# A hybrid S5 and attention block: the S5 output taken with 128 stationary columns instead of 32

## The chip, the core and the metric

The kernel runs on one core of one Trainium2 chip. The metric is the device time of one execution in microseconds, the median of several runs; shorter is better. TensorE (PE, its weight loads PEld), VectorE (DVE), ScalarE (ACT), GpSimd (POOL) and SyncE (SP, which here only issues the weight loads) each take their own instructions in order and wait for each other by semaphores.

## What is computed

One decoder block on 256 tokens of width 2048, all in float32. A modulation of six vectors is made from a conditioning vector, the input is normalised and modulated, and one projection gives u, q, k and v of 1024 channels each. u goes through a diagonal complex state space layer (S5): 64 groups of 16 channels with 64 complex states each. q, k and v go through an attention of 8 heads with three dilated windows merged. Both halves are joined in an output projection, and a SwiGLU feed forward layer follows. What matters here is the S5 layer:

```
bu = einsum('bsgc,gnc->sbgn', u, Bbar)              # complex
h[t] = abar * h[t-1] + bu[t]                        # per group and state, over 256 tokens
y = Re(einsum('sbgn,gcn->bsgc', h, C)) + d * u
y = gelu(y);  ssm_out = y * sigmoid(y @ w_glu)
```

## The kernel before

**The dense products.** Every weight matrix comes in tiles of 256 rows by 512 columns (512 KB), loaded by SyncE into a ring of six buffers (`load`, line 106) in the order of use. ScalarE casts each tile to its high part (`whi`, line 131) and VectorE subtracts to get the low part (`wlo`, line 133); there are three buffers of each. TensorE then makes three products for each piece, high by high, high by low and low by high (`mm_tok`, line 150). The modulation weights go through the same ring of raw tiles and are used uncast, by TensorE (line 225) or, for one gate and one block, by VectorE (lines 260 and 280).

**The stages.** First the modulation and u^T, then q, k, v with the S5 layer and the rest of the modulation alongside (the loop over `step()`), then the GLU of the S5 output (line 911), the output projection, the second norm, and the feed forward layer.

**The S5 layer.** It is worked in eight batches m of 128 channels, eight groups of 16. Time is cut into 64 blocks j of four tokens (four phases i or r). `U` holds the input with 4 phases x 32 channels on the 128 partitions, for each quarter Q of a batch's channels and each block j. `ssm_tables(m)` makes the constant operands of a batch. `ssm_batch(m)` does the work: TensorE brings the input to the states (`S`, line 690), ScalarE copies `S` out of PSUM (line 693), VectorE turns the states, runs the scan over the 64 blocks (line 705) and turns them back into `hp`; TensorE makes the output y from two sources, the input within the block through the triangular table `T` (line 720) and the state before the block through `Vt` (line 724); then ScalarE copies y out of PSUM (line 728) and squares it (line 729), and ScalarE and VectorE finish GELU and write the high and low parts of `yT` (lines 731 to 739). In the old form each phase r and quarter Q has a product of its own with 32 stationary columns, placed on the 32 partitions of that quarter, so that y has the channels of the batch in order on its partitions.

**Order.** The program order of the parallel stage is written out by generators: after each weight tile, `step()` advances the modulation and the lanes of S5 batches (two lanes, even and odd m) and of attention heads. The order of instructions on TensorE, VectorE, ScalarE and GpSimd is then made by the framework's planner from that program order, its priorities and its own cost model; the casts of line 131 have a raised priority. Only SyncE's order is the program's. Pools that matter: PSUM tiles `ms` have three buffers (y, S, transposes, scores), the accumulators `acc` two, and the working tiles `wk` of the S5 lanes (written by the tables and the batches) two. The tile `vt`, into which v is copied (line 785), takes the place of an earlier table tile.

Of the kernel before, what the change touches and what calls it, by code (L numbers as in the profile page):

```python
# [7 lines left out]
F32 = mybir.dt.float32  # L8
# [43 lines left out]
# columns of the array of small operands  # L52
# [9 lines left out]
def body(tc, sm, tabs, bc, brow, x, wada, wg2, win, wglu, wout, wgate, wup, wdown, out):  # L62
# [26 lines left out]
    def rsqrt(pool_, v, n, tag):  # L89
        """v [128, n] -> 1/sqrt(v) (integer first guess, Newton)"""  # L90
# [18 lines left out]
    # weights in the order of their use, split into high and low parts, read ahead  # L109
# [30 lines left out]
    def split(dst, src):  # L140
        """dst [128, ch, 2, n] f32r <- src [128, ch, n] as high and low parts"""
        A.copy(dst[:, :, 0], src)
        V.tensor_tensor(out=dst[:, :, 1], in0=src, in1=dst[:, :, 0].bitcast(F32), op=ALU.subtract)

    def mm_tok(ps, lhs, hl, j, first, last, ts_=range(2)):
        """ps [128, 2, 512] += lhs(h, t)^T @ w"""
# [5 lines left out]
    # ================= scope 1: up to the second norm =================  # L152
# [8 lines left out]
    def WK(name):  # L161
        """working tile of one S5 lane: three parts of 2 KB"""
# [14 lines left out]
    c7 = p1.tile([128, 16, 7], F32, name="c7")        # columns 3 - i .. 6 - i: c in place i  # L177
# [4 lines left out]
    sel = p1.tile([128, 4], F32, name="sel")          # place i of every quadrant  # L182
    V.reduce_sum(sel, ident.rearrange("p (q r) -> p r q", q=4)[:, 0:4], axis=AX.X)

# [5 lines left out]
    # a part: (kind, first group of 128 columns, groups); kinds shift1, scale1, gate1, shift2, scale2  # L190
# [19 lines left out]
    def ada_stream(sets):  # L210
        """generator: one tile a step; the parts of a set share a bank, and are finished while the next set runs"""
        pend = None
        for parts in sets:
            ps = ada_ps
            last = len(parts) - 1
            for i, (kind, g0, ng) in enumerate(parts):
                w = ng * 128
                nk = 1024 // w                     # groups of 128 rows in a tile
# [50 lines left out]
    def ada_dve():  # L269
        """generator: blocks of the second modulation on VectorE, one tile a step"""  # L270
# [70 lines left out]
    pw = p1.tile([128, 5, 3, 32], F32, name="pw")      # abar^0..4: re, im, -im  # L341
    rho4 = SC("rho4")
    el = p1.tile([128, 6, 2, 32], F32, name="el")      # exp(i 4 theta 2^l)
    bct = P8([128, 4, 32, 16], "bct")

    def s5_consts():
# [3 lines left out]
        def horner(o, x, cs_):  # L350
            """o = cs[0] + x (cs[1] + x (...))"""
            ts(o, x, cs_[-1], None, ALU.mult)
            for c_ in cs_[-2:0:-1]:
                stt(o, o, c_, x, ALU.add, ALU.mult)
            ts(o, o, cs_[0], None, ALU.add)
# [4 lines left out]
        def vexp(o, x, kf, r):  # L360
            """exp(x) as 2^k times a polynomial; 0 below the normal range"""
# [29 lines left out]
        tt(tmpb, tmpb, th, ALU.mult)                   # sin of the half angle  # L391
# [4 lines left out]
        ts(tmpb, tmpb, 2.0, None, ALU.mult)            # sin  # L396
        ts(tmpc, tmpc, -2.0, 1.0, ALU.mult, ALU.add)   # cos
# [6 lines left out]
        def csq(ore, oim, re, im):  # L404
            """o = (re + i im)^2"""
# [22 lines left out]
        # Bbar = ((abar - 1) / a) B  # L428
# [16 lines left out]
        ts(bct[:, 3], bct[:, 3], -1.0, None, ALU.mult)       # C as its conjugate  # L445
# [14 lines left out]
    def te_parts(m):  # L460
        """T [(i ch), Q, r, ch'] and E [e, Q, j] of the channels of m"""
# [5 lines left out]
    def ssm_rot(mp):  # L467
        """E_j = exp(i 4 theta j) of two batches"""
# [25 lines left out]
    def ssm_tables(m):  # L494
        """tables of the channels 128 m .. 128 m + 127 (4 pairs of groups)"""
# [3 lines left out]
        Bm = bct[:, 0:2, pr]                       # [128, 2, 4, 16]  # L499
        Cm = bct[:, 2:4, pr]  # L500
        wv = P8([128, 2, 4, 2, 4, 32], "wv")       # 0: W1^T [(i ch), (Q, e), state]  1: V [Q, e, tau, ch]
        wv_t[m] = wv
        wst = T4([128, 4, 2, 4, 32], "wst")        # Q, e, i, ch
        wk = WK("wkt")
        T, _ = te_parts(m)
        Tf = T.rearrange("p q r c -> p (q r c)")   # room for the steps to K
# [3 lines left out]
        Vt = wv[:, 1]                              # [128, Q, e, tau, 32]  # L510
# [3 lines left out]
        dn = wk(2, 4, 2, 4, 16)                    # Q, e, i, ch  # L514
        # W stage: block diagonal abar^(3-i) Bbar
# [9 lines left out]
        for ps_, cs_ in HV:  # L525
            A.copy(wst[ps_, :, :, :, cs_].rearrange("p q e i c -> p (q e i) c"), dn[ps_].rearrange("p q e i c -> p (q e i) c"))
            for e in range(2):
                A.copy(c0[ps_, :, e, cs_], Cm[ps_, e])             # C as its conjugate
        yield 1.6
        # V_tau, tau = 1 .. 4  # L530
# [13 lines left out]
        # K_tau = Re(C abar^tau Bbar), tau = 3 - i  # L544
# [15 lines left out]
        # Toeplitz part [(i ch), Q, r, ch'] = K_(r - i), i <= r, d on the diagonal  # L560
# [3 lines left out]
        for i in range(3):                         # r = 2: i = 0..2 <- partitions 32 (i + 1)  # L564
# [76 lines left out]
    def u_copy(b):  # L641
        """U [(i, 32 ch), m, Q, j] = u[4 j + i, 128 m + 32 Q + ch]"""
# [38 lines left out]
    def ssm_batch(m):  # L681
# [35 lines left out]
        for Q in range(4):  # L717
            yq = y[32 * Q:32 * Q + 32]
            for r in range(4):
                PE.matmul(yq[:, r], lhsT=T[:, Q, r], rhs=U[:, m, Q], start=r == 0, stop=False, skip_group_check=True,  # L720
                          tile_position=(0, 32 * Q))
            for r in range(4):
                for e in range(2):
                    PE.matmul(yq[:, r], lhsT=Vt[:, Q, e, r], rhs=hp[:, e, Q], start=False, stop=e == 1, skip_group_check=True,  # L724
                              tile_position=(0, 32 * Q))
# [504 lines left out]
```

## Time and profile before

| | |
|---|---|
| time, median of 3 runs | 1269.51 us (1268.36 to 1269.92) |
| span of the profiled execution, first to last instruction | 1262.8 us (a time of its own beside the span is not given) |
| TensorE busy | 1229.4 us (97%) |
| VectorE busy | 790.1 us (63%) |
| ScalarE busy | 569.4 us (45%) |
| GpSimd busy | 25.5 us (2%) |
| moved by DMA | 302.74 MB, mean 240 GB/s |

The busy shares are means over the whole span; a stage can have another limit than the mean shows. A busy TensorE is not TensorE at its peak, since matmuls are pipelined and their ends are modelled, so the starts of neighbouring instructions tell more than their lengths. TensorE's granted clock is at its full level from 37 us on. A float32 product with float32 operands (as S and y) is recorded as two passes, so its counts are twice those of the code.

### The profile page before, as it was taken

How to read it: one execution, taken by the hardware profiler on the slowest of the kernel's cores; microseconds unless marked ns; L12 is line 12 of the kernel's file. 1: busy time of each engine (PE TensorE's matmuls, PEld its weight loads, DVE VectorE, ACT ScalarE, POOL GpSimd, SP SyncE). 2: the span in 40 equal slices, each digit the busy share in tenths (PEclk: the TensorE clock that was granted, in tenths of full speed). 3: DMA queues.
4: the chain of work that ended last, by engine and by line, in shares of the span. 5: the costliest groups of instructions: out<-in, count | busy, mean ns of one | idle time of the engine just before them, and what ended most of it. 6: DMA issues, size and time to landing. Idle time of an engine off the chain costs nothing.

```text
span 1262.8 us, 18076 instructions
## 1 busy us (share of the span) xinstructions
PE 1229.4 (97%) x6884; PEld 961.9 (76%) x6884; DVE 790.1 (63%) x1389; ACT 569.4 (45%) x859; POOL 25.5 (2%) x50
## 2 busy tenths in 40 slices
PE   5889999999999999999999999999999999999998
PEld 2556557676789877688888888888888878888886
DVE  7994354666778999865655665665555444545443
ACT  4663363445456555554344443444434443333432
POOL 1110000000000000000000000000000000000000
PEclk9999999999999999999999999999999999999999
DMA  9889967767687899567777777777766656767662
GB/s 376 268 294 350 347 217 266 249 235 260 219 323 237 264 333 326 203 190 240 240 240 229 233 247 232 238 238 226 244 199 192 187 166 197 208 194 212 191 211 67
DMA packets 83032, 302.74 MB, mean 240 GB/s; under 512 B 9248, under 2 KB 9664, under 8 KB 82304
## 3 DMA queue, kind: packets, MB, share of 16 engines
q1 hardware_dynamic: 80784, 294.69, 71.6%
q10 hardware_dynamic: 1728, 4.38, 0.9%
q0 software_dynamic: 432, 2.51, 0.5%
q8 instruction: 54, 0.88, 0.3%
q14 instruction: 34, 0.28, 0.1%
HBM read 299.44 MB, written 2.10 MB: 239 GB/s over the span
## 4 chain that ended last, share of the span: by engine, by line
PE 83%; DVE 8%; DMA 5%; issue 2%; ACT 2%; DVEq 0%; ACTq 0%
PE ff L150 38%; PE dn L150 14%; PE qkv L150 9%; PE ada L225 5%; PE dnl L150 5%; DMA raw<-wada 4%; PE uacc L600 3%; DVE wlo L133 2%; PE y L724 2%; DVE gate L260 1%; PE q L150 1%; PE S L690 1%; PE y L720 1%; PE atp L1106 1%; ACT whi L131 1%
## 5 line engine op out<-in xcount | busy, mean ns | idle before, releaser
L133 DVE TENSOR_TENSOR wlo<-raw,whi 128x1024 fp32r<-128x1024 f32 x365 | 445.6, 1222 | 323.4 <-ACT whi L131 322.4
L131 ACT CAST whi<-raw 128x1024 fp32r<-128x1024 f32 x365 | 384.3, 1053 | 517.8 <-PE ff L150 263.7
L150 PE MATMUL ff<-whi,h2T 128*128 128x512 f32 x1408 | 437.1, 390 | 0.7 <-DVE h2T L1026 0.5
L150 PEld LDWEIGHTS ff<-whi,h2T 128*128 128x128 f32 x1408 | 264.0, 188 | 56.8 <-ACT h2T L1025 1.0
L150 PE MATMUL ff<-wlo,h2T 128*128 128x512 f32 x704 | 274.1, 389 | 0.0
L150 PE MATMUL dn<-whi,aT 128*128 128x512 f32 x528 | 163.4, 390 | 0.0
L150 PEld LDWEIGHTS ff<-wlo,h2T 128*128 128x128 f32 x704 | 132.2, 188 | 27.0
L150 PEld LDWEIGHTS dn<-whi,aT 128*128 128x128 f32 x528 | 99.1, 188 | 21.1 <-ACT whi L131 0.2
L150 PE MATMUL qkv<-whi,hT 128*128 128x512 f32 x320 | 107.7, 402 | 0.0
L150 PE MATMUL dn<-wlo,aT 128*128 128x512 f32 x264 | 103.1, 391 | 0.0
L225 PE MATMUL ada<-raw,c 128*4 128x256 f32 (+1 forms) x736 | 87.5, 467 | 14.7 <-DVE c L179 9.8
L150 PEld LDWEIGHTS qkv<-whi,hT 128*128 128x128 f32 x320 | 60.0, 188 | 25.9 <-issue 9.9
L1084 DVE SCALAR_TENSOR_TENSOR gate<-raw,cs,gate 128x1024 f32<-128x1024 f32 x32 | 41.1, 1284 | 53.5 <-DMA raw<-wg 53.5
L150 PE MATMUL qkv<-wlo,hT 128*128 128x512 f32 x160 | 63.3, 395 | 0.0
L600 PE MATMUL uacc<-hT,whi 128*128 128x256 f32 x256 | 53.0, 300 | 4.7 <-ACT whi L131 2.3
L150 PEld LDWEIGHTS dn<-wlo,aT 128*128 128x128 f32 x264 | 49.6, 188 | 10.6 <-issue 0.5
L150 PE MATMUL dnl<-whi,aT 128*128 128x512 f32 x176 | 54.5, 389 | 0.0
L600 PEld LDWEIGHTS uacc<-hT,whi 128*128 128x128 f32 x256 | 40.8, 195 | 17.5 <-issue 8.8
L260 DVE SCALAR_TENSOR_TENSOR gate<-raw,cs,gate 128x512 f32<-128x512 f32 x64 | 47.7, 747 | 5.0 <-DMA raw<-wada 4.5
L225 PEld LDWEIGHTS ada<-raw,c 128*4 128x4 f32 x736 | 12.8, 85 | 44.6 <-issue 17.4
L600 PE MATMUL uacc<-hT,wlo 128*128 128x256 f32 x128 | 38.1, 298 | 1.6 <-DVE wlo L133 1.6
L150 PEld LDWEIGHTS dnl<-whi,aT 128*128 128x128 f32 x176 | 33.0, 188 | 7.1 <-DVE o L333 0.2
(312 smaller groups left out, 1259.2 us busy)
## 6 DMA issues: line engine op xcount, KB each, us to landing
raw<-wada SPq DMA_DIRECT2D x160, 512.0 KB, 5.2
raw<-wgate SPq DMA_DIRECT2D x88, 512.0 KB, 4.4
raw<-wup SPq DMA_DIRECT2D x88, 512.0 KB, 4.3
raw<-wdown SPq DMA_DIRECT2D x88, 512.0 KB, 4.2
raw<-win SPq DMA_DIRECT2D x64, 512.0 KB, 5.0
raw<-wout SPq DMA_DIRECT2D x32, 512.0 KB, 4.6
raw<-wg SPq DMA_DIRECT2D x32, 512.0 KB, 4.3
raw<-wglu SPq DMA_DIRECT2D x8, 512.0 KB, 4.7
```

What stands on the lines that cost most here:

```text
L131: A.copy(hi, raw)
L133: V.tensor_tensor(out=lo, in0=raw, in1=hi.bitcast(F32), op=ALU.subtract)
L150: PE.matmul(ps[t] if type(ps) is list else ps[:, t], lhsT=lhs(a, t), rhs=w[:, j], start=first and n == 0, stop=last and n == 2)
L225: PE.matmul(ps[32 * q:32 * q + 4, 0:w], lhsT=c7[:, kc, 3 - i:7 - i], rhs=wt[:, j * w:(j + 1) * w], start=i == 0 and kc < 4, stop=i == last ...
L260: V.scalar_tensor_tensor(out=gb, in0=wt[:, j], scalar=cs[:, 2 * h + j:2 * h + j + 1], in1=gb, op0=ALU.mult, op1=ALU.add)
L600: PE.matmul(uacc[b][:, c], lhsT=wt[:, j, w], rhs=h[:, j, a], start=(kc == 0 and n == 0 and c % 2 == 0), stop=(kc == 15 and n == 2), skip_g ...
L690: PE.matmul(S[:, e, Q], lhsT=wv[:, 0, Q, e].rearrange("p i c -> p (i c)"), rhs=U[:, m, Q], start=True, stop=True)
L720: PE.matmul(yq[:, r], lhsT=T[:, Q, r], rhs=U[:, m, Q], start=r == 0, stop=False, skip_group_check=True, tile_position=(0, 32 * Q))
L724: PE.matmul(yq[:, r], lhsT=Vt[:, Q, e, r], rhs=hp[:, e, Q], start=False, stop=e == 1, skip_group_check=True, tile_position=(0, 32 * Q))
L1084: V.scalar_tensor_tensor(out=g, in0=wt, scalar=cs[:, k:k + 1], in1=g, op0=ALU.mult, op1=ALU.add)
L1106: PE.transpose(tp[:, k, t * 128:(t + 1) * 128], sg[:, t, (k2 * 2 + k) * 128:(k2 * 2 + k + 1) * 128], ident)
```

## The change

Comments are removed, and in `ssm_batch` the S5 output is made and copied in another way:

```diff
         y = ms([128, 4, 64], "y")
         for Q in range(4):
-            yq = y[32 * Q:32 * Q + 32]
-            for r in range(4):
-                PE.matmul(yq[:, r], lhsT=T[:, Q, r], rhs=U[:, m, Q], start=r == 0, stop=False, skip_group_check=True,
-                          tile_position=(0, 32 * Q))
-            for r in range(4):
-                for e in range(2):
-                    PE.matmul(yq[:, r], lhsT=Vt[:, Q, e, r], rhs=hp[:, e, Q], start=False, stop=e == 1, skip_group_check=True,
-                              tile_position=(0, 32 * Q))
+            PE.matmul(y[:, Q], lhsT=T[:, Q].rearrange("p r c -> p (r c)"), rhs=U[:, m, Q], start=Q == 0, stop=False, skip_group_check=True)
+            for e in range(2):
+                PE.matmul(y[:, Q], lhsT=Vt[:, Q, e].rearrange("p r c -> p (r c)"), rhs=hp[:, e, Q], start=False, stop=e == 1,
+                          skip_group_check=True)
         ysb, t1 = wk(1, 64, 4), wk(2, 64, 4)
-        A.copy(ysb, y.rearrange("p r j -> p j r"))
+        for r in range(4):
+            for Q in range(4):
+                A.copy(ysb[32 * Q:32 * Q + 32, :, r], y[32 * r:32 * r + 32, Q])
         A.activation(t1, ysb, AF.Square)
```

The four phases of a quarter are now one stationary operand of 128 columns (the tables lie that way already), so a product gives 4 phases x 32 channels on the partitions, and the quarter goes into the free dimension. Per batch 48 products become 12. Since the steps behind want the channels on the partitions and the phase next to the block, the one ScalarE copy of 128 partitions by 256 becomes 16 copies of 32 partitions by 64, each from the 32 partitions of phase r to the 32 partitions of quarter Q, written with a stride of four elements. Everything after the copies is unchanged, and so is the order in which the program issues the stages.

## Rows read from the trace of the kernel before

**Rows 1.** The chain of work that ended last, of the whole kernel: its shares by engine, then by line.

```profile
PE 83%; DVE 8%; DMA 5%; issue 2%; ACT 2%; DVEq 0%; ACTq 0%
PE ff L150 38%; PE dn L150 14%; PE qkv L150 9%; PE ada L225 5%; PE dnl L150 5%; DMA raw<-wada 4%; PE uacc L600 3%; DVE wlo L133 2%; PE y L724 2%; DVE gate L260 1%; PE q L150 1%; PE S L690 1%; PE y L720 1%; PE atp L1106 1%; ACT whi L131 1%
```

**Rows 2.** The three stretches around the change: start and end in us, its length, busy time of PE, PEld, DVE, ACT and POOL, each with its number of instructions, the granted TensorE clock (1.00 is full speed), the busy share of the DMA engines and what they moved.

```profile
178.00:385.00 207.00, 206.99 (x1658) 150.08 (x1657) 137.98 (x363) 97.45 (x232) 8.09 (x13) 1.00 0.72 252
385.00:525.00 140.00, 137.17 (x719) 113.60 (x718) 129.18 (x227) 75.83 (x121) 0.53 (x1) 1.00 0.85 289
525.00:1263.00 738.00, 732.41 (x3264) 604.07 (x3262) 406.64 (x381) 307.04 (x320) 0.50 (x1) 1.00 0.68 208
```

**Rows 3.** The TensorE passes that make the S5 output y: count, duration in ns (least/median/most), first and last start in us, form of the operands.

```profile
L724 PE MATMUL y<-wks,wv x512: 219/219/243, 204.0 to 378.2; 128*32 128x64 f32 x171
...
L720 PE MATMUL y<-U,te x256: 219/219/243, 203.5 to 377.3; 128*32 128x64 f32 x128
```

**Rows 4.** TensorE in order of time, around one S product and around the second pair of S5 outputs: start and length in us, line, operation, number of instructions merged.

```profile
229.76 2.00 PE L690 MATMUL S<-U,wv 128*128 128x64 f32 x16
231.57 0.47 PE L150 MATMUL qkv<-whi,hT 128*128 128x512 f32 x1
...
252.32 0.61 PE L720 MATMUL y<-U,te 128*32 128x64 f32 x8
...
261.78 0.50 PE L150 MATMUL qkv<-whi,hT 128*128 128x512 f32 x1
```

**Rows 5.** ScalarE: four groups of instructions by form (busy us, mean ns of one, idle time before), and then two places of its order of time.

```profile
L646 ACT COPY U<-uacc 32x256 f32<-32x256 f32 x22 | 8.0, 364 | 1.7 <-PE uacc L600 1.4
...
L693 ACT COPY wks<-S 128x512 f32<-128x512 f32 x8 | 4.7, 586 | 7.2 <-PE S L690 7.2
...
L524 ACT COPY wkt<-bct 128x64 f32<-128x64 f32 x16 | 3.3, 242 | 2.4 <-DVE te L333 1.6 <-DVE yT L739 0.7
...
L728 ACT COPY wks<-y 128x256 f32<-128x256 f32 x8 | 3.0, 371 | 17.8 <-PE y L724 17.8
...
177.06 0.74 ACT L646 COPY U<-uacc 32x256 f32<-32x256 f32 x2
...
266.66 0.39 ACT L524 COPY wkt<-bct 128x64 f32<-128x64 f32 x2 [0.66 <-DVE yT L739]
```

**Rows 6.** After the first two S5 outputs: ScalarE, then VectorE, then TensorE, each in order of time.

```profile
220.56 0.36 ACT L728 COPY wks<-y 128x256 f32<-128x256 f32 x1
...
224.18 1.04 ACT L131 CAST whi<-raw 128x1024 fp32r<-128x1024 f32 x1
...
226.82 1.20 DVE L133 TENSOR_TENSOR wlo<-raw,whi 128x1024 fp32r<-128x1024 f32 x1
...
231.89 0.39 PE L150 MATMUL qkv<-wlo,hT 128*128 128x512 f32 x1
```

**Rows 7.** During and after the second pair of S5 outputs: ScalarE, then VectorE, then TensorE, each in order of time.

```profile
254.44 1.05 ACT L131 CAST whi<-raw 128x1024 fp32r<-128x1024 f32 x1 [4.29 <-DMA raw<-win]
...
261.89 0.37 ACT L728 COPY wks<-y 128x256 f32<-128x256 f32 x1 [3.77 <-PE y L724]
262.30 0.42 ACT L729 ACTIVATE wks<-wks 128x256 f32<-128x256 f32 x1
...
266.73 0.36 DVE L333 TENSOR_TENSOR wkt<-pw,bct 128x192 f32<-128x192 f32 x1
...
274.47 1.21 DVE L133 TENSOR_TENSOR wlo<-raw,whi 128x1024 fp32r<-128x1024 f32 x1
...
276.38 0.48 PE L150 MATMUL qkv<-wlo,hT 128*128 128x512 f32 x1
```

**Rows 8.** During and after the third pair: ScalarE, then TensorE, each in order of time.

```profile
316.06 0.37 ACT L728 COPY wks<-y 128x256 f32<-128x256 f32 x1 [4.33 <-PE y L724]
...
319.84 0.42 ACT L738 ACTIVATE yT<-wks 128x256 fp32r<-128x256 f32 x1 [1.31 <-DVE wks L735]
322.57 0.37 ACT L728 COPY wks<-y 128x256 f32<-128x256 f32 x1 [2.31 <-PE y L724]
322.84 1.02 ACT L785 COPY vt<-qkv 128x1024 f32<-128x1024 f32 x1
...
324.01 2.22 PE L690 MATMUL S<-U,wv 128*128 128x64 f32 x18
326.04 0.47 PE L150 MATMUL qkv<-whi,hT 128*128 128x512 f32 x1
```

**Rows 9.** After the last pair: ScalarE, then VectorE, then TensorE, each in order of time.

```profile
370.88 1.09 ACT L131 CAST whi<-raw 128x1024 fp32r<-128x1024 f32 x1
...
378.42 0.37 ACT L728 COPY wks<-y 128x256 f32<-128x256 f32 x1 [3.77 <-PE y L724]
...
379.15 1.25 ACT L777 ACTIVATE qkT<-qtp,smt 128x512 f32<-128x512 f32 x2
...
382.21 1.05 ACT L131 CAST whi<-raw 128x1024 fp32r<-128x1024 f32 x1 [0.26 <-PE qkv L150]
384.93 1.05 ACT L131 CAST whi<-raw 128x1024 fp32r<-128x1024 f32 x1 [1.67 <-PE qkv L150]
...
383.30 1.23 DVE L133 TENSOR_TENSOR wlo<-raw,whi 128x1024 fp32r<-128x1024 f32 x1 [0.89 <-ACT whi L131]
...
387.92 0.59 PE L911 MATMUL z<-yT,whi 128*128 128x256 f32 x2
```

## Prediction

> **What bounds the kernel now.** I read the chain of waits first. 83% of the chain that ends last is TensorE, and by line two thirds of the whole are the dense products through line 150; the two lines of the S5 output, 720 and 724, stand in it with 1% and 2% [rows 1]. So TensorE time taken off there should count, if TensorE is the limit in that stage. The table of stretches answers that. From 178 to 385 us, where the q, k, v products run with the S5 layer beside them, TensorE is busy 206.99 of 207 us, VectorE 138 and ScalarE 97. From 385 to 525 us (GLU, output projection) VectorE is busy 129 of 140 us and the DMA engines 0.85 of the time; afterwards TensorE leads again [rows 2]. The granted clock is 1.00, the 2.4 GHz level, in all three, so a pass has the same price before and after. All edits lie in the first stretch: the first S5 output pass starts at 203.5 and the last at 378.2 us [rows 3].
>
> One more thing is to be seen before costing: ScalarE and VectorE take their instructions in order, and the casts of line 131 and the subtractions of line 133, which make the high and low parts of each weight tile for TensorE, stand in the same queues as the S5 work. ScalarE has room on average (97 of 207 us), but what counts is how late a cast may come at four places: after the first two batches, which come singly, and after each of the three pairs of batches.
>
> **Removed: 96 passes per batch.** An S5 output in the old form is 16 products with T and 32 with V per batch, recorded as two passes each: 512 + 256 passes for eight batches [rows 3]. The second pair shows the price undisturbed: its first pass starts at 252.32 and the next product at 261.78, 9.46 us for 192 passes, 0.0493 us each [rows 4]. Eight batches: 768 x 0.0493 = 37.8 us.
>
> **Added: 24 passes per batch.** New are 4 products with T and 8 with V, each with 128 stationary columns and 64 moving ones. This form is in the trace: the S products of line 690 are 128x128 against 128x64, and 16 such passes take from 229.76 to 231.57, 0.113 us each [rows 4]. If a pass cost only as much as an old one, 0.0493, eight batches would take 9.5 us; I see no reason for that, since the identical form has a row. Eight batches: 192 x 0.113 = 21.7 us. TensorE is given 37.8 - 21.7 = **16.1 us**, 2.0 per batch, 4.0 per pair.
>
> The Trainium skill speaks against the change here: its page "TensorEngine Tiling (Array Packing)", section "Theoretical Speedup", gives up to 4x to products with 32 columns, when four tiles are at work. By it the old form would cost no more than the new, and the change would save TensorE nothing. The trace agrees only in direction and excludes the rest: a narrow pass is 2.3 times cheaper (0.0493 against 0.113 [rows 4]), but there are four times as many, and the order takes all 24 passes of one quarter before the next.
>
> **Added: 15 ScalarE copies per batch.** One copy of 128x256 (0.371 us) becomes 16 of 32x64 out of PSUM [rows 5]. No row has that form. Copies out of PSUM cost 0.371 us at 256 and 0.586 at 512 columns, 0.84 ns a column, so 64 columns come to 0.210 us. Neighbouring copies on changing partitions don't overlap: two of line 646 take 0.74 at 0.364 each, whereas two of line 524 on the same partitions take 0.39 at 0.242 [rows 5]. In the new loop the partitions change with each copy. I take 0.223 us a copy (0.210 and the 0.012 between those of line 646): 3.57 per batch, 3.2 more than now, 25.6 in all. Bounds: 0.15 a copy, if they overlap as those of line 524 do (2.4 per batch), and 0.377, a whole step of line 646 (6.0 per batch).
>
> The Trainium skill, page "ScalarE: Activation LUTs", section "What ACT_TABLE_LOAD costs", states 186 ns and 0.833 ns a column, with an overlap of about 93 ns between neighbours: an estimate of 0.146 us a copy, 2.3 per batch; by it the losses below would shrink by about 1.2 us per batch where the copies are late. The rows of line 646 show no such overlap, and I go by them.
>
> The average hides this work: ScalarE would have 123 of some 191 us. What is not hidden is that the S5 chain, and all that is queued behind it, is later. The copies sit in ScalarE's queue ahead of the square, the tanh and the next casts. I move each place by the rows, with TensorE 2.0 us earlier per batch and the copies 3.57 long.
>
> *First two batches* [rows 6]. They give 4.0 us. The first batch's copies run beside TensorE's next products; the second's push the cluster that ends with the cast at 224.18 by 3.2, from a start that is 4.0 earlier. The low part (subtraction at 226.82, 1.2 long) comes at 227.2 instead of 228.0; TensorE wants it at 231.89 - 4.0 = 227.9. It just fits, and the tiles behind it follow closely; lost: 0.3 us.
>
> *Second pair* [rows 7]. The first output would be ready at 255.0, its copies run after the cast at 254.44 from 255.5 to 259.1, then the square (0.42), the second set to 263.0, its square to 263.5. Today that square ends at 262.72. So although TensorE is 4.0 earlier, the chain behind it is 0.7 later. What waits for it: working buffers are two, and the tables for the last two batches (line 333, at 266.73) start only when the batches are finished with theirs. From there VectorE runs nearly without a gap to the subtraction at 274.47, whose low part TensorE takes at 276.38, 0.7 us after it is written (274.47 + 1.21). Lost: 4.0 + 0.7 - 0.7 = 4.0, about the whole gain of this pair.
>
> *Third pair* [rows 8]. The v copy of line 785 (at 322.84, 1.02 long) stands behind the last output and must end before the products at 326.04 can reuse its accumulator. TensorE would be there at 322.0. With the queue as it stands, the first output's copies run from 313.6 (2.4 before today's, whose output has eight passes of the second batch ahead of it) to 317.2; what stands between them and the second set, up to the scaling of line 738, takes 3.4 to 3.8 today, so the second set ends at about 324.2 and the v copy at 325.2 (lost 3.2). If the v copy follows the second output (ready at 318.3) and its copies at once, it ends at 322.9 (lost 0.9). I take 2.0.
>
> *Last pair* [rows 9]. The passes would run from 368.9 (9.46 before the copy at 378.42) to 374.3. The first copies start behind the cast of 370.88, at 372.0; two sets and a square end at 379.6. Then come square, two qkT copies, tanh and scalings as now, 3.1 us: the cast of 382.21 would be at 382.7, its subtraction done at 385.0, while TensorE wants the high part at 387.92 - 4.0 = 383.9 and the low part within half a us. Lost: about 1.0.
>
> *The rest.* The banks of the outputs stay taken some 3 us longer; in the rows above no TensorE instruction comes early enough after a pair to need them, so I put nothing. Loads: the bytes are the same in some 5% less time; the stretch has its DMA engines busy 0.72 of the time [rows 2], and would have 0.76. The later stretches get the same work at the same rates and shift.
>
> **Sum.** 16.1 - (0.3 + 4.0 + 2.0 + 1.0) = 8.8 us. The page gives 1262.8 us as the span and no time of the whole execution; the median of the runs, 1269.5, lies 6.7 above it, and since start and end are untouched I take the sum off the median: **1261 us**.
>
> **Rivals.** *One: the whole gain.* The queues are rearranged by a planner that knows the copies; it may put casts, the first batch's tanh and the v copy between them, or the copies overlap at 0.15 (second pair: chain 1.6 earlier instead of 0.7 later). For it: ScalarE has half its time free. Against it: 0.7 us at line 133 leaves no room [rows 7]. Time: 1269.5 - 16.1 = 1253.4. Chance 0.24.
>
> *Two: handed back.* TensorE arrives earlier everywhere and waits: 4.0 lost at each of the last two pairs, 4.7 at the second, 2 at the first batches, as the old ends of the S5 chains stay. Time: 16.1 - 14.7 = 1.4 less, 1268.1. For it: the chain after a pair is no earlier in my own count. Against it: the casts after the last pair wait for TensorE today (1.67 us at 384.93 [rows 9]), not the reverse. Chance 0.14.
>
> *Three: slower, by the price of a copy.* If 32 partitions at a stride cost a full step of line 646, 0.377, a pair's chain is 10 us more ScalarE than now. The second pair's square then ends at 268.4 (lost 5.7 + 4.0 - 0.7 = 9.0), the v copy at 328.7 (lost 6.7), the cast after the last pair at 387.4 (lost 5.5), and the first two batches give back their 4.0. Sum: 25.2 - 16.1 = 9.1 more, 1278.6. Between -8.8 at 0.223 and +9.1 at 0.377 the sign changes near 0.30 us a copy. Against it: line 646 moves four times as many columns. A poor new order of the queues at the second pair would act the same way. Chance 0.14.
>
> **How the numbers follow.** My forecast (1256 to 1266) has 0.48. The range takes in rival one and reaches into two: 1253 to 1270; above it lie rival three and a little more. A change of 0.2%, 2.5 us, is about what can be told from none. Faster by more: forecast and rival one, 0.72. Within: 0.14. Slower: 0.14.
>
> **What would show it.** Right: 24 passes per batch at 0.11 us and a pair in about 5.4 us; 128 copies of 32x64 near 0.21 us, spaced 0.22; TensorE idle, or its order changed, ahead of a low part of line 133 after the second pair, and ahead of the block that follows the v copy; the GLU starting 7 to 11 us earlier than 387.92 [rows 9]; the stretch after it as long as now. Wrong: passes dearer than 0.113 (each 0.01 costs 1.9 us); copies at 0.3 or more; VectorE's tables after the second pair starting 3 us earlier, which would be rival one; or a longer stretch from the GLU to the second norm, which my sum has unchanged.

## The result: 0.6% slower, and the profile after

The changed kernel takes 1276.49 us (median of four runs, 1273.52 to 1279.23) against 1269.72 us for the kernel before beside it: ratio 1.0060, 95% interval 1.0043 to 1.0077. The forecast was 1261 us, faster; it was wrong in sign, and the time lies above the range.

The profiled execution of the changed kernel is the quickest of the four, 1273.52 us with a span of 1271.7. Lines behind the products stand two lower than in the kernel before: the T products are line 718, the Vt products 720, the copies 726, the square 727, the v copy 783, the GLU 909. The first stretch of [rows 2], in the same columns:

```profile
178.00:385.00 207.00, 198.83 (x1059) 133.66 (x1058) 133.32 (x353) 117.92 (x324) 8.04 (x13) 0.97 0.69 244
```

In the first stretch TensorE was busy all the time before; now it is idle for 8 us, and its mean clock is 0.97 instead of 1.00. The new instructions, as count, duration in ns (least/median/most), first and last start, form:

```profile
L720 PE MATMUL y<-wks,wv x128: 275/275/476, 206.0 to 382.7; 128*128 128x64 f32 x128
L726 ACT COPY wks<-y x128: 248/265/273, 212.4 to 392.4; 32x64 f32<-32x64 f32 x128
...
L718 PE MATMUL y<-U,te x64: 217/275/421, 205.8 to 382.2; 128*128 128x64 f32 x64
```

192 passes and 128 copies, as the change says. Some passes last 476 ns instead of 275: the slow clock. Now the four places of the prediction. ScalarE, then TensorE, after the second pair [rows 7]:

```profile
256.84 4.69 ACT L726 COPY wks<-y 32x64 f32<-32x64 f32 x17 [5.84 <-PE y L720]
...
261.81 1.65 ACT L726 COPY wks<-y 32x64 f32<-32x64 f32 x6
263.49 1.04 ACT L131 CAST whi<-raw 128x1024 fp32r<-128x1024 f32 x1
...
253.91 0.43 PE L718 MATMUL y<-U,te 128*128 128x64 f32 x2
...
259.29 0.47 PE L150 MATMUL qkv<-whi,hT 128*128 128x512 f32 x1
...
264.58 0.51 PE L150 MATMUL qkv<-whi,hT 128*128 128x512 f32 x1 [1.31 <-ACT whi L131]
265.85 0.51 PE L150 MATMUL qkv<-wlo,hT 128*128 128x512 f32 x1 [0.76 <-DVE wlo L133]
```

The pair's 48 passes take 5.38 us (253.91 to 259.29). Then ScalarE makes 23 copies before it comes to a cast; the cast of the same weight tile was done in the kernel before at 254.44 [rows 7], ahead of any copy. TensorE waits 2.07 us for its high and low parts. At the third pair [rows 8], ScalarE and then TensorE, and last a TensorE row of the kernel before from the same place:

```profile
317.24 4.39 ACT L726 COPY wks<-y 32x64 f32<-32x64 f32 x16 [1.55 <-PE y L720]
...
321.69 0.69 PE L690 MATMUL S<-U,wv 128*128 128x64 f32 x2 [2.82 <-ACT wks L726]
...
316.60 0.78 PE L690 MATMUL S<-U,wv 128*128 128x64 f32 x6
```

In both kernels S products stand just behind the first output of this pair, ahead of most of the second. S needs a PSUM tile of the pool that y uses. In the kernel before, the one copy of the first output ends at 316.43 [rows 8] and S starts 0.17 us later, without a wait. In the changed kernel the copies hold the tile to the end of the sixteenth, and TensorE waits 2.82 us. After the waits at the second and the third pair the clock falls. The columns are those of [rows 2], for the 3.8 us with the first wait, the stretch behind them, the second wait and the stretch behind it:

```profile
263.00:266.80 3.80, 1.74 (x9) 1.00 (x6) 1.23 (x1) 3.65 (x12) 0.00 (x0) 1.00 0.51 139
266.90:270.30 3.40, 3.40 (x10) 2.02 (x10) 2.60 (x6) 2.43 (x6) 0.00 (x0) 0.51 0.78 299
318.80:321.50 2.70, 0.07 (x1) 0.00 (x0) 0.40 (x3) 2.58 (x11) 0.00 (x0) 1.00 1.05 378
321.60:331.70 10.10, 10.01 (x37) 7.80 (x38) 2.47 (x8) 4.44 (x12) 0.00 (x0) 0.50 0.32 103
```

TensorE was busy 1.74 of 3.80 us, and then its granted clock is 0.51, the 1.2 GHz level, for 3.4 us; it stood still for 2.7 us, and then the clock is 0.50 for 10.1. TensorE is busy all that time, so half of it is lost: 6.8 us. The last pair [rows 9], ScalarE and then TensorE:

```profile
380.30 3.87 ACT L726 COPY wks<-y 32x64 f32<-32x64 f32 x14 [2.83 <-PE y L720]
...
387.48 3.58 ACT L726 COPY wks<-y 32x64 f32<-32x64 f32 x13
391.09 1.04 ACT L131 CAST whi<-raw 128x1024 fp32r<-128x1024 f32 x1
...
392.18 0.50 PE L150 MATMUL qkv<-whi,hT 128*128 128x512 f32 x1 [1.11 <-ACT whi L131]
393.44 0.50 PE L150 MATMUL qkv<-wlo,hT 128*128 128x512 f32 x1 [0.76 <-DVE wlo L133]
...
396.57 0.59 PE L909 MATMUL z<-yT,whi 128*128 128x256 f32 x2
```

Again copies (30 in all, with the scalings of q between them), and only then the cast that stood at 370.88 before. The GLU starts at 396.57 instead of 387.92 [rows 9], 8.65 later; the whole profiled execution ends 8.96 later. The first q, k, v product already starts 1.30 us later (178.09 instead of 176.79), before any edited line has run. So 7.35 us are lost between there and the GLU.

**Where those 7.35 us are.** I count each TensorE pass from its start to the start of the next one, with waits and the share lost at half clock taken out, from the first q, k, v product to the GLU (211.13 us before, 218.48 after). The S5 output takes 17.45 us less. Against it stand 10.32 us of waits, 6.76 us of half clock, 1.95 us in the q, k, v products, and 5.89 us in the modulation passes (`ada`, line 225), which are the same 196 passes in both kernels but take 37.03 us instead of 31.14; the rest is 0.12 us less. TensorE at the first output, before and then after:

```profile
203.51 0.60 PE L225 MATMUL ada<-raw,c 128*4 128x512 f32 x2
203.52 0.63 PE L720 MATMUL y<-U,te 128*32 128x64 f32 x8
203.94 0.60 PE L225 MATMUL ada<-raw,c 128*4 128x512 f32 x2
203.99 0.39 PE L724 MATMUL y<-wks,wv 128*32 128x64 f32 x4
204.47 0.50 PE L150 MATMUL qkv<-wlo,hT 128*128 128x512 f32 x1
...
204.81 1.03 PE L225 MATMUL ada<-raw,c 128*4 128x512 f32 x4
205.77 0.43 PE L718 MATMUL y<-U,te 128*128 128x64 f32 x2
```

Four modulation passes together with twelve narrow y passes took 0.96 us before; four modulation passes alone take 0.96 now. A group of them among full-width products takes 0.95 to 0.97 us at full clock, whether it has two passes or eight. So it costs something when they lose their narrow neighbours, and when the new order splits a group. In the profiled executions of all kernels with the new products they take 34.6 to 38.1 us.

**Time with the clock taken out.** Each run lists the mean granted clock of its span. Time multiplied by that clock is what it would be at the full level if TensorE set every microsecond (an estimate). Four runs of the changed kernel: 1273.52 at 0.993, 1275.26 at 0.992, 1277.73 and 1279.23 at 0.989; the products are 1263.7 to 1265.2, mean 1264.6. The runs of the kernel before beside the experiments, at 0.9975 to 0.998, give means of 1264.7 to 1265.6. By this estimate the change gains and loses nothing at full clock, and the loss of 7 us is the clock's; the profiled execution, with 6.8 us in this stage, agrees. The mean clock of a run is not this stage's alone, though: other profiled executions have falls where no S5 output is made (partitions in another order at 53, 73, 118 and 534 us).

### The profile page after: what moved, and what is told of

Read it like the earlier page. It is cut to its first block, busy times and chain, and to the rows that moved or that the text cites. A ratio compares the mean times of both kernels' runs of the same rounds, so it can differ in the third digit from the quotient of the medians.

```text
span 1271.7 us, 17046 instructions
## 1 busy us (share of the span) xinstructions
PE 1226.3 (96%) x6308; PEld 950.3 (75%) x6308; DVE 790.8 (62%) x1389; ACT 599.6 (47%) x979; POOL 25.5 (2%) x50
## 4 chain that ended last, share of the span: by engine, by line
PE 85%; DVE 5%; ACT 4%; DMA 4%; issue 2%; DVEq 0%; SPq 0%; ACTq 0%
PE ff L150 38%; PE dn L150 14%; PE qkv L150 8%; PE ada L225 5%; PE dnl L150 5%; PE uacc L600 3%; DMA raw<-wada 2%; ACT wks L726 2%; PE z L909 2%; DVE wlo L133 2%; PE q L150 2%; PE wo L150 2%; PE wol L150 1%; ACT whi L131 1%; PE S L690 1%
## 5 line engine op out<-in xcount | busy, mean ns | idle before, releaser
L150 PE MATMUL qkv<-whi,hT 128*128 128x512 f32 x320 | 110.5, 409 | 2.4 <-ACT whi L131 2.4
L225 PE MATMUL ada<-raw,c 128*4 128x256 f32 (+1 forms) x736 | 92.3, 470 | 14.4 <-DVE c L179 9.5
L150 PEld LDWEIGHTS qkv<-wlo,hT 128*128 128x128 f32 x160 | 30.7, 192 | 13.5 <-DVE wlo L133 4.8
L726 ACT COPY wks<-y 32x64 f32<-32x64 f32 x128 | 33.9, 265 | 13.6 <-PE y L720 12.1
```

Of the source, the lines that this page charges most:

```text
L150: PE.matmul(ps[t] if type(ps) is list else ps[:, t], lhsT=lhs(a, t), rhs=w[:, j], start=first and n == 0, stop=last and n == 2)
L225: PE.matmul(ps[32 * q:32 * q + 4, 0:w], lhsT=c7[:, kc, 3 - i:7 - i], rhs=wt[:, j * w:(j + 1) * w], start=i == 0 and kc < 4, stop=i == last ...
L726: A.copy(ysb[32 * Q:32 * Q + 32, :, r], y[32 * r:32 * r + 32, Q])
```

## The experiments

Four theories stood at the start or came up on the way. **A**: the block of copies in ScalarE's queue makes casts late and holds banks; TensorE waits, and its clock falls after the waits. **B**: the new products themselves, or the order the planner makes around them. **C**: the clock falls because the new S5 output gives TensorE less to do, whatever the copies. **D**: it is the length of the S5 chain that counts, whichever engine does the copies. Ratios are against the kernel before run with each (1267.66 to 1269.04 us).

**One copy again (changed kernel, the move to channel order left out).**

```diff
-        for r in range(4):
-            for Q in range(4):
-                A.copy(ysb[32 * Q:32 * Q + 32, :, r], y[32 * r:32 * r + 32, Q])
+        A.copy(ysb, y.rearrange("p q j -> p j q"))
```

> The full-width products of the changed kernel, but one ScalarE copy of 128x256 instead of the 16; the move back to channel order is left out. Theory A (the 16 copies on ScalarE cost the time, through late casts, a PSUM bank held too long, and the clock falls that follow TensorE's waits): 8 to 16 us faster than the kernel before, 1253 to 1261, the granted clock at its full level from 40 us on, TensorE's waits between 178 and 400 us gone except for the subtractions after the second pair. Theory B (it is the new products and the new order of the queues, whatever follows them): 1270 or more, with the wait ahead of the S product near 319 us and a half clock behind it. Theory C (TensorE's clock falls because the new S5 output gives it less to do): faster than the changed kernel by the copies, but with clock falls near 267 and 322 us as there.

Measured: 1257.41 us, ratio 0.9914 (0.9899 to 0.9928). The stretch from 178 to 385 us:

```profile
178.00:385.00 207.00, 206.61 (x1178) 146.11 (x1174) 146.67 (x388) 105.08 (x244) 8.05 (x13) 1.00 0.76 265
```

TensorE is busy nearly all the time at full clock, with the new products. C falls, and of B the products: without the 16 copies they gain 10.3 us, and the GLU of this profiled execution starts 12.7 earlier than before. The order that the planner makes around the copies is not tested here.

**The copies alone (kernel before, its one copy replaced by 16 of the same size, from and to the same partitions).**

```diff
-        A.copy(ysb, y.rearrange("p r j -> p j r"))
+        for r in range(4):
+            for Q in range(4):
+                A.copy(ysb[32 * Q:32 * Q + 32, :, r], y[32 * Q:32 * Q + 32, r])
```

> The 32-column products of the kernel before, followed by 16 ScalarE copies of 32x64 (same partitions in and out) instead of one. Theory A: copies of 0.265 us, 0.276 apart, 4.1 us more ScalarE per batch; with TensorE giving nothing back the time is 4 to 12 us above the kernel before, 1274 to 1282, with the same waits after the pairs. Theory B: within 2.5 us of the kernel before. Theory C: slower by at most the few us of the late casts, no fall of the clock, since the old passes keep TensorE occupied.

Measured: 1278.43 us, ratio 1.0088 (1.0072 to 1.0105).

```profile
178.00:385.00 207.00, 204.99 (x1637) 145.89 (x1634) 133.47 (x356) 120.75 (x333) 8.18 (x13) 1.00 0.71 249
...
L730 ACT COPY wks<-y x128: 243/265/273, 212.9 to 387.9; 32x64 f32<-32x64 f32 x128
```

The copies cost 10.8 us with the old products, at the price they have in the changed kernel, as A forecast. But A's waits after the pairs did not come, TensorE's longest wait in this stretch is 0.72 us, and the clock does not fall, as C had expected of the old products. The profiled execution is 5.1 us late at the GLU and 9.8 at the feed forward layer, so half of the price falls behind the GLU, where the changed kernel loses 0.3 us. 10.8 - 10.3 leaves 0.5, and the changed kernel loses 7. That the rest is the clock is argued from its size (6.8), not shown: the two kernels lose their time in different places.

**Partitions in another order (changed kernel, Q outside, r inside).**

```diff
-        for r in range(4):
-            for Q in range(4):
+        for Q in range(4):
+            for r in range(4):
```

> The changed kernel with its two copy loops exchanged: four copies in a row write the same 32 partitions. If copies that write the same partitions overlap, as the two of line 524 do (0.15 apart), three of four steps shrink from 0.276 to about 0.17, a batch takes 3.2 us instead of 4.4, and by theory A the time falls by 2 to 6 us below the changed kernel's 1276. If they stay 0.276 apart, the partitions are not what keeps them from overlapping, and the time is within 3 us of the changed kernel by all theories.

Measured: 1276.54 us, ratio 1.0061 (1.0038 to 1.0083); the copies start 0.277 us apart. Four neighbours now write the same partitions, and nothing overlaps. That the written partitions change is not the reason; the partitions read still change with each copy here, and what decides stays open.

**Quarters inside (kernel before, its 32-column products in another order).** Its one copy stays.

```diff
-        for Q in range(4):
-            yq = y[32 * Q:32 * Q + 32]
-            for r in range(4):
+        yq = [y[32 * Q:32 * Q + 32] for Q in range(4)]
+        for r in range(4):
+            for Q in range(4):
...
-            for r in range(4):
-                for e in range(2):
+        for r in range(4):
+            for e in range(2):
+                for Q in range(4):
```

> The kernel before with its 48 products per batch in another order, the quarter innermost, so that neighbouring passes go to different column groups; one copy as before. If column groups work side by side (the modulation's passes with 4 columns start in such groups of four), the 96 passes take 1.2 to 2.7 us per batch instead of 4.7, TensorE gets 16 to 28 us and ScalarE nothing more: by theory A 1250 to 1262. If they do not, the passes stay 0.049 apart and the time is within 2.5 us of the kernel before. By theory C the shorter S5 output brings clock falls with it and the gain is under 5 us.

Measured: **1247.19 us, ratio 0.9845 (0.9821 to 0.9870)**, the quickest of all. TensorE around the second pair:

```profile
248.96 0.63 PE L720 MATMUL y<-U,te 128*32 128x64 f32 x32
...
251.75 0.50 PE L150 MATMUL qkv<-whi,hT 128*128 128x512 f32 x1
```

The passes of [rows 4] that took 9.46 us a pair run from 248.96 to 251.75, counted in the same way: 2.79 us for 192 passes, 0.0145 each, 3.4 times as fast as in the old order, and 1.9 times as fast as the 48 new ones (5.38). When neighbours go to different 32 columns, they work side by side; the kernel before sent some 20 in a row to the same 32. The time is 3 us below the range expected; the passes took 1.4 us per batch, inside theirs.

**Every second copy on VectorE (changed kernel).**

```diff
-                A.copy(ysb[32 * Q:32 * Q + 32, :, r], y[32 * r:32 * r + 32, Q])
+                (V.tensor_copy if Q % 2 else A.copy)(ysb[32 * Q:32 * Q + 32, :, r], y[32 * r:32 * r + 32, Q])
```

> The changed kernel with every second of the 16 copies on VectorE. Theory A (length of the copy block in ScalarE's queue): the block falls from 4.4 to about 2.2 us where VectorE is free, so more than half of the distance between the changed kernel (1276) and the one with a single copy (1257) is won back: 1258 to 1267. Rival D (not the queue of ScalarE but the length of the S5 chain itself decides, whichever engine does the copies): the chain shortens only as far as both engines really run side by side; VectorE is busy for most of the time after the second pair, so 1266 to 1276.

Measured: 1260.06 us, ratio 0.9932 (0.9910 to 0.9953).

```profile
L726 ACT COPY wks<-y x64: 246/265/278, 211.3 to 380.4; 32x64 f32<-32x64 f32 x64
L726 DVE COPY wks<-y x64: 257/268/280, 211.6 to 380.9; 32x64 f32<-32x64 f32 x64
...
211.91 0.26 ACT L726 COPY wks<-y 32x64 f32<-32x64 f32 x1 [0.33 <-DVE wks L726]
212.20 0.26 DVE L726 COPY wks<-y 32x64 f32<-32x64 f32 x1 [0.33 <-ACT wks L726]
...
256.86 1.04 ACT L131 CAST whi<-raw 128x1024 fp32r<-128x1024 f32 x1
257.93 0.38 ACT L726 COPY wks<-y 32x64 f32<-32x64 f32 x2
```

No copy is quicker, and the block is not half as long: the copies of a batch wait for each other across the two engines and start about 0.29 us apart. On average a square starts 11.2 us after the last pass of its output, against 7.0 in the changed kernel. So A's number came, but not by the way it gave. What did change is the place of the casts, which now stand between the copies: the one that had 23 copies ahead of it at the second pair has six, ends at 257.90, and TensorE comes to its tile at 259.25 without a wait. TensorE idles 3.1 us up to the GLU instead of 10.3, and its clock stays full in this stretch. D falls, not only by its range: the chain is the longest here, and most of the gain is back.

**Rows together (changed kernel, copies write 64 neighbouring elements; the last two steps of GELU put the phases in place).**

```diff
-        ysb, t1 = wk(1, 64, 4), wk(2, 64, 4)
+        ysb, t1 = wk(1, 4, 64), wk(2, 4, 64)
...
-                A.copy(ysb[32 * Q:32 * Q + 32, :, r], y[32 * r:32 * r + 32, Q])
+                A.copy(ysb[32 * Q:32 * Q + 32, r], y[32 * r:32 * r + 32, Q])
```

> The changed kernel with the copied y kept as phase by block, so that each copy writes 64 elements in a row; the last two steps put the phases in order. If the stride of the write makes a copy of 32x64 take 0.265 instead of the 0.210 worked out before, it falls to about 0.21 and the block to 3.6 us: 1268 to 1274. If 0.265 is what a small copy from PSUM to other partitions takes in any case: 0.26 to 0.27 again and a time within 3 us of the changed kernel's.

Measured: 1268.80 us (ten runs), ratio 1.0005 (0.9989 to 1.0021).

```profile
L726 ACT COPY wks<-y x128: 188/203/208, 214.4 to 383.6; 32x64 f32<-32x64 f32 x128
...
319.41 0.43 PE L690 MATMUL S<-U,wv 128*128 128x64 f32 x2 [1.86 <-ACT wks L726]
```

The stride of four in the write costs 62 ns a copy; without it they start 0.215 us apart. That is the price I had forecast, and the time is still not below that of the kernel before: S waits 1.86 us. The lower price gives about 7 us; it was only one of the failed steps.

**Staged (changed kernel, one copy to SBUF, then the 16 from there), and the same 16 on GpSimd.**

```diff
+        yst = wk(2, 2, 4, 64)[:, 1]
+        A.copy(yst, y)
...
-                A.copy(ysb[32 * Q:32 * Q + 32, :, r], y[32 * r:32 * r + 32, Q])
+                A.copy(ysb[32 * Q:32 * Q + 32, :, r], yst[32 * r:32 * r + 32, Q])
```

> The changed kernel with one more ScalarE copy: y leaves PSUM at once in a copy of 128x256 (0.37 us), and the 16 copies go from there. The bank is free after 0.4 us, the block is 0.4 us longer. If the PSUM bank (the S product that waited 2.8 us at 319 us, and the half clock for 10 us after it) is the main cause of the loss: 1266 to 1271, no wait ahead of that S product, no fall near 322 us. If the late casts are: 1276 to 1281, with the waits after the second and the last pair as long as before.

Measured: 1278.81 us, ratio 1.0083 (1.0056 to 1.0111). The copies, and TensorE after the second pair:

```profile
L728 ACT COPY wks<-wks x128: 287/302/313, 214.7 to 391.1; 32x64 f32<-32x64 f32 x128
...
267.65 0.49 PE L150 MATMUL qkv<-whi,hT 128*128 128x512 f32 x1 [2.47 <-ACT whi L131]
```

The bank is free after 0.37 us and no S waits for it, but the block is longer (copies 0.313 us apart), and the casts and the v copy come later: waits of 2.47 us for a cast, 4.97 for the v copy and 2.49 for a cast at the three pairs. Freeing the bank, with a block that is 1 us longer, gives nothing back.

> As the staged form, but the 16 copies run on GpSimd, which is busy 2% of the time; ScalarE has one copy per batch as in the kernel before. Theory A (ScalarE's queue): the casts are early again and the time goes to 1256 to 1263 even if GpSimd takes up to 0.3 us a copy. Rival D (length of the chain): the block of 16 is as long or longer, the tables after the second pair start as late as in the changed kernel or later, and the time stays at 1268 to 1280.

Measured with `G.tensor_copy` in place of `A.copy` for the 16: 1283.45 us, ratio 1.0118 (1.0098 to 1.0138). After the copies' own row, what ScalarE's square waited for in all (us, times), then ScalarE and TensorE after the second pair:

```profile
L728 POOL COPY wks<-wks x128: 286/292/1365, 213.1 to 397.0; 32x64 f32<-32x64 f32 x128
...
  POOL wks L728: 36.1, 8
...
274.46 0.42 ACT L729 ACTIVATE wks<-wks 128x256 f32<-128x256 f32 x1 [5.93 <-POOL wks L728]
...
275.89 1.03 ACT L131 CAST whi<-raw 128x1024 fp32r<-128x1024 f32 x1
...
276.97 0.79 PE L150 MATMUL qkv<-whi,hT 128*128 128x512 f32 x1 [5.73 <-ACT whi L131]
```

The time lies above the ranges of both theories. ScalarE is rid of the work and loses its time all the same, 36.1 us in eight waits of the square, and a cast that TensorE needs stands behind such a square: TensorE waits 5.73 us. A in its narrow form, ScalarE's busy time, falls. What remains, and fits the kernel with half the copies on VectorE too, is the place of the casts: all that a cast has ahead of it in ScalarE's queue counts, waits for another engine included.

**Casts first (changed kernel, planner's priority of the casts raised).**

```diff
-HP = 60
+HP = 150
```

> The changed kernel with one number altered: the raised priority of the casts of line 131 goes from 60 to 150. The same altered number leaves the order of the kernel before as it was but for a few instructions, so it has no price of its own there. In the changed kernel the planner now puts the cast that stood behind 17 + 6 copies after the second pair in front of the second set of copies; the work itself is the same, 128 copies at 0.276. If late casts are what makes TensorE wait, then the gaps after the second pair (2.07 us before two products of tile 39) shrink to under 0.5 us, the half clock that follows in the changed kernel has less cause, and the time falls below the changed kernel's 1276.5 by 3 to 8: 1268 to 1273. If the length of the S5 chain itself counts and not the casts' place in the queue (the tables of the next batches and the banks come as late as before), it stays at 1275 to 1279.

Measured: 1269.42 us (ten runs, 1265.47 to 1274.46), ratio 1.0006 (0.9989 to 1.0024): inside the interval expected if late casts count. The profiled execution is the slowest of the ten. ScalarE after the second pair, then TensorE:

```profile
265.28 1.05 ACT L131 CAST whi<-raw 128x1024 fp32r<-128x1024 f32 x1
...
266.67 4.40 ACT L726 COPY wks<-y 32x64 f32<-32x64 f32 x16
...
271.41 1.03 ACT L131 CAST whi<-raw 128x1024 fp32r<-128x1024 f32 x1
...
272.49 0.49 PE L150 MATMUL qkv<-whi,hT 128*128 128x512 f32 x1 [1.10 <-ACT whi L131]
273.75 0.50 PE L150 MATMUL qkv<-wlo,hT 128*128 128x512 f32 x1 [0.77 <-DVE wlo L133]
```

The gap did not shrink as expected (1.87 us): one cast went ahead of the second set, the next now stands behind it. The same work in another order of the queues is worth 7 us. In this execution TensorE idles 7.5 us up to the GLU instead of 10.3: S waits 1.52 us instead of 2.82, and after the last pair 1.4 us are waited instead of 2.8, while the low part after the first two batches costs 1.89 instead of 0.84. The ten runs also show the clock: the quickest, 1265.47 at 0.996, and the slowest, 1274.46 at 0.989, have the same product, 1260.4.

**All together.** From the profiled execution of each kernel: the time from the last pass of an output to its square (mean of eight batches), and TensorE's idle time from the first q, k, v product to the GLU. From all its runs: the median, the mean clock, and the mean of time multiplied by clock.

| kernel | output to square, us | TensorE idle, us | median us | clock | time x clock |
|---|---|---|---|---|---|
| before (7 runs) | 1.0 | 0.0 | 1267.66 | 0.998 | 1265.3 |
| quarters inside | 2.3 | 2.4 | 1247.19 | 0.9965 | 1243.9 |
| one copy | 1.4 | 0.4 | 1257.41 | 0.9965 | 1252.5 |
| half on VectorE | 11.2 | 3.1 | 1260.06 | 0.9965 | 1255.4 |
| rows together | 5.8 | 4.9 | 1268.80 | 0.9935 | 1260.1 |
| casts first | 8.2 | 7.5 | 1269.42 | 0.993 | 1261.4 |
| changed | 7.0 | 10.3 | 1276.49 | 0.991 | 1264.6 |
| staged | 8.3 | 11.3 | 1278.81 | 0.9885 | 1264.1 |
| GpSimd | 8.8 | 15.8 | 1283.45 | 0.987 | 1266.5 |
| copies alone | 6.0 | 2.0 | 1278.43 | 0.997 | 1274.4 |

Among the kernels with the new products (the rows from one copy to GpSimd) the time follows TensorE's idle time, not the time from the output to the square, and the clock falls with it, from 0.9965 to 0.987. The share of the clock is an estimate by the product in the last column: no kernel kept the waits and held the clock up.

## Why the prediction was wrong

*What bounds the kernel.* Right: with one copy the shorter passes came out as time, 10.3 of the 16.1 us. A term was missing: the modulation passes that ran among the narrow y passes. They take 3.5 us more with one copy and 5.9 in the changed kernel.

*Removed and added passes.* Right: forecast 0.113 us a pass and 5.4 a pair, measured 5.38 for 48.

*Price of a copy: mis-sized.* 0.223 forecast, 0.276 measured, inside my bounds. The row I scaled from writes neighbouring elements; that form measures 0.203 long and 0.215 apart against my 0.210 and 0.223. The stride of the write, which I named only under rival three, is the difference. By my own line from -8.8 at 0.223 to +9.1 at 0.377, 0.276 gives -2.6: this term explains 6.2 of the 15.6 us between the forecast (-8.8) and the result (+6.8); the rows-together kernel, at 0.215 apart, gives about 7 of them back.

*The four places.* I measure each by the starts of the same weight tiles in both traces. The changed kernel is 1.30 us late before the first output (204.38 against 203.08), 2.55 early after the first two (219.39, 221.94), 1.49 late before the second pair (249.99, 248.50), 3.91 late after it (287.72, 283.81), 8.73 late before the last pair (374.75, 366.02) and 8.65 late at the GLU. The first two outputs gave 3.85 us, and each pair 4.08 (9.46 less 5.38, measured at the second), 16.1 as forecast. So the places lost 4.0, 6.5, 8.9 and 4.0 us, 23.4 in all; forecast were 0.3, 4.0, 2.0 and 1.0, 7.3 in all.

*First two batches: 0.3 forecast, 4.0 lost.* I had written that the low part just fits. TensorE waits 0.84 us for it at 231.31, and from there to the second pair the new order has seven groups of modulation passes in place of four, at 0.95 us or more a group.

*Second pair, 4.0 forecast and 6.5 lost; last pair, 1.0 and 4.0.* The step that failed is one sentence each: that the copies run after the cast at 254.44 and start behind the cast of 370.88. I held the places of the casts as they were in the queue, and added the copies behind them. The planner put these casts behind 23 and 30 copies. The prediction says of rival three that a poor new order at the second pair would act the same way, and gave it no price.

*Third pair: 2.0 forecast, 8.9 lost; the largest error.* I followed the v copy and put the bank at nothing: "in the rows above no TensorE instruction comes early enough after a pair to need them, so I put nothing". The rows did not hold the place that mattered, inside the pair: the kernel before has S products at 316.60, 0.17 us after the copy of the first output ends, so 4.4 us of copies in place of 0.37 had to hold them up. They waited 2.82 us, and the half clock behind that wait cost another 5.1.

*The clock.* "A pass has the same price before and after" failed. The full clock of before was that of a TensorE that never stood still in this stretch [rows 2]; once it waits, that is no longer given. 6.8 us in the profiled execution, 1.7 behind the second pair's wait and 5.1 behind the third's; both are in the losses above.

*The rest.* Right for this change: from the GLU on both kernels run alike (8.65 late there, 8.96 at the end), and no wait between the first output and the GLU ends with a load.

*The rivals.* Rival three had the sign and nearly the time (1278.6), but its cause, copies above 0.30 us, did not come: at 0.276 the price should have left a gain. That the time came near its figure is chance. (Its 10 us more ScalarE for a pair should be 11.3: 32 copies at 0.377 less two of 0.371.) Rival two, handed back, has the size of what happened at full clock, by the estimate.

*The rule I set aside.* I wrote that the trace excludes a gain from narrow passes side by side. It did not. It showed an order in which some 20 passes in a row use the same 32 columns, and where one quarter gives way to the next, the last Vt passes of the one alternate with the first T passes of the other:

```profile
253.50 0.22 PE L724 MATMUL y<-wks,wv 128*32 128x64 f32 x1
253.53 0.22 PE L720 MATMUL y<-U,te 128*32 128x64 f32 x1
253.55 0.22 PE L724 MATMUL y<-wks,wv 128*32 128x64 f32 x1
```

These start 0.03 us apart, those within a quarter 0.056. My 0.0493 was a mean over both, and I missed it. With the quarters inside the same passes are 3.4 times as fast, and the 32-column form was the one to keep. The Trainium skill, "TensorEngine Tiling (Array Packing)", section "Theoretical Speedup", gives up to 4x for it.

I also set aside an overlap of neighbouring copies, and the 16 copies of a batch show none: on ScalarE they start 11 or 12 ns after the one before ends. Only where half of them ran on VectorE did ScalarE do two copies of 0.265 us in 0.38 us. The Trainium skill, "ScalarE: Activation LUTs", section "What ACT_TABLE_LOAD costs", states an overlap of about 93 ns between neighbours.

## What to carry to other kernels

Work put on a half-idle engine is not hidden if that engine also feeds the limiting one in order: follow each feeding instruction (here the casts) and ask what stands ahead of it in its queue in the new order, not in the old one. When a PSUM tile is held longer, look for the next writer of that pool inside the stage, not only behind it. Every place where TensorE would wait also puts its clock at risk. Before trading narrow products for wide ones, try the order in which neighbours use different columns of the array. When a small operation has no row, ask of the nearest row whether it reads and writes in the same pattern.

## What was not expected of the hardware

- TensorE's clock at 0.50 for 10.1 us behind a standstill of 2.7 us, and at 0.51 for 3.4 us behind 3.8 us in which it was busy 1.74; yet not after the waits of 1.11 and 0.76 us at 391. What decides, and how long the fall lasts, stays open.
- Modulation passes with 4 columns: a group among full-width products takes 0.95 to 0.97 us for two, four or eight passes; four of them took no longer together with twelve passes on 32 columns.
- Products on 32 columns: 0.0145 us a pass where neighbours use different columns, 0.0493 where they use the same.
- ScalarE copies of 32x64: 0.203 us from PSUM to neighbouring elements, 0.265 at a stride of four elements, 0.302 from SBUF at that stride; VectorE 0.268 from PSUM, GpSimd 0.292 from SBUF.
